# Attention output of an encoder block turned by VectorE and passed through HBM, in place of TensorE transposes

## The chip, the cores and the metric

The kernel runs on one core of a Trainium2 chip. The metric is the device time of one execution in microseconds; the time of the kernel before is the median of three runs. TensorE (PE in the profile) multiplies matrices, VectorE (DVE), ScalarE (ACT) and GpSimd (POOL) work on tiles in SBUF and PSUM, and SyncE (SP) issues the loads and stores. Each engine takes its instructions in the order of the program and waits on semaphores for the others.

## What is computed

One layer of a hybrid encoder, 1024 tokens by 1024 channels, all in float32. Cut to what bears on the change:

```
h    = rmsnorm(x);  proj = h @ w_in                  # 1024 x 5664
q, k, v, r, lr_f, lr_b, u, g_a, g_b = split(proj)
o    = gla(q, k, v, fwd) + gla(reversed, bwd)        # 4 heads, 128 keys, 256 values each
o    = o * rsqrt(mean(o*o over a head's 256 values) + EPS)
o    = o (heads side by side: 1024 x 1024) * gla_norm
o    = o * silu(r)
y_a  = o @ w_branch_gla
y_b  = pooling mixer of u
x    = x + (sigmoid(g_a)*y_a + sigmoid(g_b)*y_b) @ w_out
x    = x + swiglu ffn(rmsnorm(x));  return rmsnorm(x)
```

## The kernel before

Every float32 operand of a large product is split into a high and a low part, and a product is three matmuls (`products`, L273): high by high, high by low, low by high. `split_to` makes the parts: the cast of the high part on ACT (L200), the difference on POOL or DVE (L201). Weights are loaded as `raw` or `fraw` and become `wh` and `wl`. The larger products are cut further, in the manner of Strassen, into seven products p1 to p7 per pair of blocks (`Unit`, `Gates`): sums of weight blocks (`fs`, L1093, on DVE) are multiplied by sums of activation blocks. The latter lie in HBM (`f_out`), are reloaded as `hs` (L673) and split into `trh` (ACT, L707) and `trl` (DVE, L698).

The order of the work is written by hand, engine by engine. PE works through the large products; after each three matmuls `pump` moves generators on by what the matmuls are worth, so the attention's small steps stand between them. A value that a generator yields is how much PE work lies until its next step.

**Attention of a head** (`attention(h)`) first makes the decays (L822 onwards). Then come the backward states, then the output loop over eight chunks of 128 tokens (NT = 8, tokens on the partitions). A chunk's output bank `op` gets its terms on PE, the last of them from the forward state `sf` (L998). The state is brought on meanwhile by `advance`: `kv` on PE, `st` on DVE (L913), `sf` and `so` on ACT (L917, L921). DVE copies `op` into the SBUF tile `o` (L999; two tiles, four chunks of 256 values each), and ACT squares and sums it (L1000). After the last chunk `rms_scale` makes all eight chunks' scales `ors` (an addition on DVE, L304, a power on POOL). `normalize` (L1019), eight TENSOR_SCALAR, runs from the list `unscaled` at the next head's decay, and the two tiles are then put on the list `deferred`, from which `flush` (L563) issues stores to `o_out`. The last head is normalized at once and stays in SBUF.

**Behind the attention** PE makes the six first blocks of r (j = 0 to 5, two halves of 512 tokens each; channels on the partitions, tokens along the free axis). `load_o` (L1033) brings heads 0 to 2 back as `ol` at j = 2, 3 and 4. `gated(j, half, ...)` needs o with channels on the partitions. It takes silu of r on ACT (`sr`, L1185), turns four 128x128 blocks of o on PE into a PSUM bank `tp` (L1188), and DVE multiplies the bank by the gla_norm column and `sr` (L1195). The first three blocks of r are put by, so from j = 3 on each half gates two of them. Finished blocks go out to `ob_out`. Blocks 6 and 7 of r are gate unit 0, made in seven products in the order p1, p2, p6, p5, p3, p7, p4; p1, p6 and others share the PSUM bank `u`, which ACT or DVE take into `ga` (L1474 copies, L1479 adds) before PE goes on in it. `gated` of these two blocks stands further back, between them and the next units.

Of the kernel before, what the change touches and what calls it, by code (L numbers as in the profile page):

```python
# [10 lines left out]
F32 = mybir.dt.float32  # L11
# [4 lines left out]
ALU = mybir.AluOpType  # L16

P = 128
# [3 lines left out]
NT = SEQ // P  # L22
HALF = 512
HEADS = 4
DK = 128
DV = 256
RANK = 16
CH = 128
SUB = 64
GROUPS = 4  # L30
WINDOWS = (2, 4, 8, 16)
PAD = 8
# [21 lines left out]
def kernel(  # L54
# [20 lines left out]
    nc = tc.nc  # L75
# [10 lines left out]
    ps_g = ctx.enter_context(tc.tile_pool(name="ps_g", bufs=8 - MM_BANKS, space=bass.MemoryType.PSUM))  # L86

    dram = ctx.enter_context(tc.tile_pool(name="dram", bufs=1, space=bass.MemoryType.DRAM))
# [8 lines left out]
    def slot(dtype=F32, shape=(2, HALF), s="slot"):  # L97
        return slots.tile([P, *shape], dtype, tag="slot", name=name(s))
# [10 lines left out]
    def bank(pool, s="ps"):  # L109
        return pool.tile([P, HALF], F32, tag=pool.name, name=name(s))  # L110
# [5 lines left out]
    ident = const.tile([P, P], F32, tag="ident", name="ident")  # L116
# [185 lines left out]
    def rms_scale(ms, width, s):  # L302
        rs = vec(width, s)
        nc.vector.tensor_scalar(rs[:, :], ms, EPS, None, op0=ALU.add)  # L304
        nc.gpsimd.tensor_tensor(rs[:, :], rs[:, :], half_neg[:, :width], op=ALU.pow)
        return rs
# [132 lines left out]
    g_mix, g_ffn, g_gla, g_pool = (cols[:, 8 * i : 8 * i + 8] for i in range(4))  # L439
# [116 lines left out]
    deferred = []  # L556

    def later(dst, src):
        deferred.append((dst, src))

    def flush(eng=nc.sync):
        while deferred:
            eng.dma_start(*deferred.pop(0))  # L563
# [167 lines left out]
            aside.pop(0)  # L731


    o_heads, unscaled = {}, []
    HOLD, SCORES = 5.0, 6

    class ValueWeights:
# [75 lines left out]
    def attention(h):  # L813
# [16 lines left out]
        for run in runs:  # L830
            nc.scalar.activation(zs[run][:, :], zs[run][:, :], AF.Exp, scale=-1.0)
        if unscaled:
            unscaled.pop()()
        yield 3.5
        flush()
        for run in runs:
            nc.scalar.activation(zs[run][:, :], zs[run][:, :], AF.Ln, bias=1.0)
# [107 lines left out]
        q, k = qk_heads[h]  # L945
# [21 lines left out]
        for n in range(NT - 1, 0, -1):  # L967
            m = n - 1
# [9 lines left out]
        p = scores(0)  # L978
# [3 lines left out]
        o = [slot(shape=(4, DV), s="o") for _ in range(2)]  # L982
        ms = vec(NT, "oms")
        old = sf = None
        for n in range(NT):
            half, i = n // 4, n % 4
            op = bank(ps_g, "op")
            products(op[:, :DV], tokens(p, n), value(n), last=False)
            terms = []
            if n < NT - 1:  # L990
                terms.append((chunk_of(qe, n, 1), sb[half][:, i, :]))
            if n > 0:
                terms.append((chunk_of(qe, n, 0), sf[:, :]))
            for j, (a, b) in enumerate(terms):
                if j == len(terms) - 1 and n < NT - 1:
                    sf = s1((DV,), "sf")
                    old = advance(old, n, 0, kts[half, 0], sf[:, :], n == NT - 2)
                nc.tensor.matmul(op[:, :DV], a, b, start=False, stop=j == len(terms) - 1)  # L998
            nc.vector.tensor_copy(o[half][:, i, :], op[:, :DV])  # L999
            nc.scalar.activation(  # L1000
                op[:, DV:], op[:, :DV], AF.Square, scale=1.0 / 16.0, accum_out=ms[:, n : n + 1]
            )
            if n == 0:
                yield 0.38
                kts[1, 0] = transposed_keys(1, 0)
            if n == 1:
                yield 0.75
                q_next = scores(1)
            if n == 3:
                p = q_next  # L1010
            yield 1.02
        rs = rms_scale(ms[:, :], NT, "ors")
        if h == HEADS - 1:
            o_heads[h] = o

        def normalize():
            for n in range(NT):
                t = o[n // 4][:, n % 4, :]
                nc.vector.tensor_scalar(t, t, rs[:, n : n + 1], None, op0=ALU.mult)  # L1019
            if h < HEADS - 1:  # L1020
                for half in range(2):
                    later(o_out[h][:, 4 * half : 4 * half + 4, :], o[half][:, :, :])

        unscaled.append(normalize)
        if h == HEADS - 1:
            unscaled.pop()()

    o_out = [dram.tile([P, NT, DV], F32, name=f"o_out{h}") for h in range(HEADS - 1)]

    def load_o(h):  # L1030
        o_heads[h] = [slot(shape=(4, DV), s="ol") for _ in range(2)]
        for half in range(2):
            nc.sync.dma_start(o_heads[h][half][:, :, :], o_out[h][:, 4 * half : 4 * half + 4, :])  # L1033

    def sums_behind():
        prepare_beside(map(feature_sums, range(2)), 2)
# [145 lines left out]
    def gated(j, half, src):  # L1182

        sr = t2(s="sr")
        nc.scalar.activation(sr[:, :], src, AF.Silu)  # L1185
        tp = bank(ps_g, "tp")
        for i in range(4):
            nc.tensor.transpose(  # L1188
                tp[:, i * P : (i + 1) * P],
                o_heads[j // 2][half][:, i, (j % 2) * P : (j % 2 + 1) * P], ident[:, :],  # L1190
            )
        if j // 2 not in oT:
            oT[j // 2] = [slot(s="o") for _ in range(2)], []
        tiles, there = oT[j // 2]
        nc.vector.scalar_tensor_tensor(  # L1195
            tiles[half][:, j % 2, :], tp[:, :], g_gla[:, j : j + 1], sr[:, :], op0=ALU.mult, op1=ALU.mult
        )
        there.append((j, half))
        if len(there) == 4:
            c = j // 2 % 2  # L1200
            for half, t in enumerate(tiles):
                later(ob_out[j // 4, half][:, 2 * c : 2 * c + 2, :], t[:, :, :])
            soon(2, flush)
# [8 lines left out]
    for j in range(KT - 2):  # L1212
        if 2 <= j <= 4:
            load_o(j - 2)
        w = take()
        if j == 4:
            for _ in range(2):
                gunits[0].load()
        if j == 5:
            gates_ahead.step()  # L1220
        if j < BY:
            whole_r = slot(s="r")
        for half in range(2):
            if j >= BY and not sums_begun and (j > BY or not side):
                finish_side()
                finish_beside()
                prepare_beside([feature_parts()], 5)
                sums_begun = True
            ps = feature_major(w, hT, half)
            if half == 0:  # L1230
                flush()
            elif j == KT - 3:
                for _ in range(2):
                    gunits[1].load()
            if j < BY:
                nc.scalar.copy(whole_r[:, half, :], ps[:, :])
                raw_r.append((j, half, whole_r[:, half, :]))
            else:
                put_by()
                gated(j, half, ps[:, :])  # L1240
            if j == KT - 3 and half == 0:
                gates_ahead.step()
# [187 lines left out]
    def pooling():  # L1430

        for g in range(GROUPS):
            u = [t2(HALF + 2 * PAD, s="u") for _ in range(2)]
# [555 lines left out]
    scales = {}  # L1989
# [74 lines left out]
    for at, p in enumerate(OUT_ORDER):  # L2064
# [9 lines left out]
        for i in range(CLOSE if closing else n_of):  # L2074
            n = at * n_of + i
# [57 lines left out]
```

## Time and profile before

| | us |
|---|---|
| median of three runs | 1374.98 (1374.72 to 1375.22) |
| span of the profiled execution | 1373.4 |
| PE busy | 1361.4 |
| VectorE busy | 836.8 |
| ScalarE busy | 647.3 |
| GpSimd busy | 752.1 |
| DMA, mean busy share of 16 engines | 53.8% |

The profile is that of one execution. Its own time is its span and some 1.6 us around it, taking the median for it. The profile lists instructions as start, length, engine, line, operation, tile written and tiles read; "x2" joins two in a row, and square brackets show how long the engine had been idle and who released it. PE's lengths overlap: how much of PE a matmul takes is seen from one start to the next.

### The profile page before, as it was taken

How to read it: one execution, taken by the hardware profiler on the slowest of the kernel's cores; microseconds unless marked ns; L12 is line 12 of the kernel's file. 1: busy time of each engine (PE TensorE's matmuls, PEld its weight loads, DVE VectorE, ACT ScalarE, POOL GpSimd, SP SyncE). 2: the span in 40 equal slices, each digit the busy share in tenths (PEclk: the TensorE clock that was granted, in tenths of full speed). 3: DMA queues.
4: the chain of work that ended last, by engine and by line, in shares of the span. 5: the costliest groups of instructions: out<-in, count | busy, mean ns of one | idle time of the engine just before them, and what ended most of it. 6: DMA issues, size and time to landing. Idle time of an engine off the chain costs nothing. (4 is left out here: it accounts for less than half of the span.)

```text
span 1373.4 us, 17879 instructions
## 1 busy us (share of the span) xinstructions
PE 1361.4 (99%) x6310; PEld 1132.9 (82%) x6310; DVE 836.8 (61%) x1034; ACT 647.3 (47%) x1177; POOL 752.1 (55%) x557
## 2 busy tenths in 40 slices
PE   9999999999999999999999999999999999999998
PEld 7888888888888888888888888888888888888886
DVE  6974556554735777678883955655566556343375
ACT  7365666755534445554346533333333334444253
POOL 3323723222597547667764376666676667455454
PEclk9999999999999999999999999999999999999999
DMA  6321523314778569995416355555544447985451
GB/s 227 113 87 52 181 90 92 95 60 123 245 236 278 186 198 308 373 386 216 150 71 241 112 174 176 176 176 177 176 145 137 146 136 266 384 301 187 169 215 77
DMA packets 167834, 251.97 MB, mean 183 GB/s; under 512 B 11160, under 2 KB 94144, under 8 KB 167744
## 3 DMA queue, kind: packets, MB, share of 16 engines
q1 hardware_dynamic: 167600, 250.57, 53.8%
q8 instruction: 49, 0.80, 0.2%
q14 instruction: 41, 0.34, 0.1%
q10 hardware_dynamic: 144, 0.26, 0.0%
HBM read 168.74 MB, written 82.05 MB: 183 GB/s over the span
## 5 line engine op out<-in xcount | busy, mean ns | idle before, releaser
L201 POOL TENSOR_TENSOR wl<-fs,wh 128x512 fp32r<-128x512 f32 x124 | 173.1, 1400 | 163.5 <-ACT wh L200 104.0
L273 PE MATMUL ps<-gh,wh 128*128 128x512 f32 x616 | 240.5, 390 | 0.0
L273 PE MATMUL ps<-gl,wh 128*128 128x512 f32 x616 | 239.8, 389 | 0.3 <-DVE gl L1691 0.3
L273 PE MATMUL ps<-gh,wl 128*128 128x512 f32 x616 | 239.7, 389 | 0.0
L201 POOL TENSOR_TENSOR wl<-fraw,wh 128x512 fp32r<-128x512 f32 x93 | 134.0, 1442 | 75.0 <-ACT wh L200 72.4
L201 POOL TENSOR_TENSOR ol<-gor,oh 128x1024 fp32r<-128x1024 f32 (+1 forms) x42 | 101.3, 2417 | 86.0 <-ACT oh L200 71.7
L273 PE MATMUL ps<-hh,wh 128*128 128x512 f32 x356 | 145.1, 408 | 0.7 <-ACT ga L1474 0.7
L273 PE MATMUL ps<-hh,wl 128*128 128x512 f32 x356 | 139.0, 390 | 0.0
L273 PE MATMUL ps<-hl,wh 128*128 128x512 f32 x356 | 138.8, 390 | 0.0
L273 PEld LDWEIGHTS ps<-gl,wh 128*128 128x128 f32 x616 | 115.7, 188 | 24.5 <-DVE gl L1691 0.7
L273 PEld LDWEIGHTS ps<-gh,wh 128*128 128x128 f32 x616 | 115.7, 188 | 24.1 <-ACT hb L1710 0.2
L273 PEld LDWEIGHTS ps<-gh,wl 128*128 128x128 f32 x616 | 115.7, 188 | 23.9
L273 PE MATMUL ps<-oh,oh 128*128 128x512 f32 x308 | 119.8, 389 | 0.0
L273 PE MATMUL ps<-ol,oh 128*128 128x512 f32 x308 | 119.8, 389 | 0.0
L273 PE MATMUL ps<-oh,ol 128*128 128x512 f32 x308 | 119.8, 389 | 0.0
L201 POOL TENSOR_TENSOR wl<-wraw,wh 128x512 fp32r<-128x512 f32 x56 | 92.3, 1679 | 44.7 <-ACT wh L200 44.6
L201 POOL TENSOR_TENSOR wl<-raw,wh 128x512 fp32r<-128x512 f32 x34 | 47.4, 1404 | 108.3 <-ACT wh L200 71.9
L201 DVE TENSOR_TENSOR ol<-wor,oh 128x1024 fp32r<-128x1024 f32 (+1 forms) x42 | 62.8, 1506 | 68.1 <-ACT oh L200 55.5
L200 ACT CAST wh<-fs 128x512 fp32r<-128x512 f32 x124 | 76.1, 615 | 29.5 <-DVE fs L1093 28.3
L273 PEld LDWEIGHTS ps<-hh,wl 128*128 128x128 f32 x356 | 66.8, 188 | 14.4
L273 PEld LDWEIGHTS ps<-hh,wh 128*128 128x128 f32 x356 | 67.0, 188 | 13.1 <-ACT ga L1474 1.1
L273 PEld LDWEIGHTS ps<-hl,wh 128*128 128x128 f32 x356 | 67.0, 188 | 12.0
(281 smaller groups left out, 3073.4 us busy)
## 6 DMA issues: line engine op xcount, KB each, us to landing
fraw<-in_w_ffn_in_dram SPq DMA_DIRECT2D x44, 512.0 KB, 6.1
gor<-g_out SPq DMA_DIRECT2D x35, 512.0 KB, 6.1
fraw<-in_w_in_dram SPq DMA_DIRECT2D x22, 512.0 KB, 6.5
g_out<-s SPq DMA_DIRECT2D x44, 256.0 KB, 2.3
wor<-t_out SPq DMA_DIRECT2D x20, 512.0 KB, 3.7
raw<-in_w_in_dram SPq DMA_DIRECT2D x36, 256.0 KB, 5.1
g_out<-g SPq DMA_DIRECT2D x33, 256.0 KB, 2.6
x<-in_x_dram SPq DMA_DIRECT2D x16, 512.0 KB, 5.6
```

The costliest lines, as they stand in the source:

```text
L200: nc.scalar.copy(hi, src)
L201: eng.tensor_tensor(lo, src, as_f32(hi), op=ALU.subtract)
L273: nc.tensor.matmul(ps, a[i], b[j], start=first and n == 0, stop=last and n == 2, skip_group_check=onto)
```

## The change

The transposes leave TensorE. VectorE turns o in blocks of 32x32 with its own transpose, and the exchange of whole blocks is done by the addresses of the stores to HBM.

- In the output loop, chunk 3 is followed by `rms_scale` of the first four chunks, the end of the loop by that of the last four.
- `turn(half, part)` normalizes two chunks (two TENSOR_SCALAR of 128x256) and turns them with one transpose instruction into a tile `ot`. Half 0's two pieces stand behind chunks 5 and 6 in the loop. Half 1's stand beside the next head's decay, where `normalize` stood, with the yield of 3.5 there split into 2 and 1.5. In the last head they follow the loop.
- `o_out` now holds o with channels ahead of tokens, for all four heads. A half is stored by four DMAs of 32 partitions, and `load_o` reads a half as 128x2x512. The last head's stores are issued at j = 4, half 0, and it is reloaded at j = 5, half 0.
- `gated` reads `ol` with channels on the partitions. Tokens lie there in another order (32 by 32 interleaved), so DVE does the multiplication in four instructions of 128x4x32.

```diff
         if unscaled:
-            unscaled.pop()()
-        yield 3.5
+            unscaled.pop(0)()
+        yield 2
+        if unscaled:
+            unscaled.pop(0)()
+        yield 1.5
         flush()
...
+        def turn(half, part):
+            if part == 0:
+                turned[half] = slot(shape=(DV // SQ, 4 * SQ), s="ot")
+            two = slice(2 * part, 2 * part + 2)
+            for i in range(2 * part, 2 * part + 2):
+                t = o[half][:, i, :]
+                nc.vector.tensor_scalar(t, t, scales[half][:, i : i + 1], None, op0=ALU.mult)
+            nc.vector.transpose(
+                turned[half][:, :, :].rearrange("p k (n b) -> p n k b", b=SQ)[:, two],
+                o[half][:, two, :].rearrange("p n (k a) -> p n k a", a=SQ),
+            )
+            if part:
+                to = o_out[h][half].rearrange("(k a) (i m) -> i a k m", a=SQ, i=4)
+                for i in range(4):
+                    (last_o if h == HEADS - 1 else deferred).append((to[i], turned[half][i * SQ : (i + 1) * SQ, :, :]))
...
             if n == 3:
                 p = q_next
+                scales[0] = rms_scale(ms[:, :4], 4, "ors")
+            if n in (5, 6):
+                turn(0, n - 5)
             yield 1.02
-        rs = rms_scale(ms[:, :], NT, "ors")
+        scales[1] = rms_scale(ms[:, 4:], 4, "ors")
         if h == HEADS - 1:
-            o_heads[h] = o
...
+            turn(1, 0)
+            turn(1, 1)
+            return
+        unscaled.extend(partial(turn, 1, part) for part in range(2))
...
-            nc.sync.dma_start(o_heads[h][half][:, :, :], o_out[h][:, 4 * half : 4 * half + 4, :])
+            nc.sync.dma_start(o_heads[h][half][:, :, :], o_out[h][half].rearrange("(j p) t -> p j t", p=P))
...
-        tp = bank(ps_g, "tp")
-        for i in range(4):
-            nc.tensor.transpose(
-                tp[:, i * P : (i + 1) * P],
-                o_heads[j // 2][half][:, i, (j % 2) * P : (j % 2 + 1) * P], ident[:, :],
-            )
...
+        turned = o_heads[j // 2][half][:, j % 2, :].rearrange("p (i n b) -> p i n b", i=4, b=SQ)
+        for i in range(4):
+            nc.vector.scalar_tensor_tensor(
+                every(tiles[half][:, j % 2, :], i), turned[:, i], g_gla[:, j : j + 1], every(sr[:, :], i),
+                op0=ALU.mult, op1=ALU.mult,
+            )
...
             if half == 0:
                 flush()
+                if j == 4:
+                    deferred.extend(last_o)
+                    flush()
+                elif j == 5:
+                    load_o(HEADS - 1)
```

The order shows three places. First PE between the two halves of the sixth block of r (j = 5), where two gated operations stood; `hh` and `hl` are the parts of h, `wh` and `wl` those of the weights. Before:

```order
L273 MATMUL ps_3497<-hl_313,wh_3411 128x512
L273 MATMUL ps_3497<-hh_312,wl_3412 128x512
L1188 MATMUL tp_3538<-ident,ol_3151 128x128 x4
L1188 MATMUL tp_3546<-ident,ol_3376 128x128 x4
L273 MATMUL ps_3560<-hh_494,wh_3401 128x512
L273 MATMUL ps_3560<-hl_495,wh_3401 128x512
L273 MATMUL ps_3560<-hh_494,wl_3402 128x512
```

And in the changed program:

```order
L274 MATMUL ps_3544<-hl_313,wh_3458 128x512
L274 MATMUL ps_3544<-hh_312,wl_3459 128x512
L274 MATMUL ps_3607<-hh_494,wh_3448 128x512
L274 MATMUL ps_3607<-hl_495,wh_3448 128x512
L274 MATMUL ps_3607<-hh_494,wl_3449 128x512
```

The two rows of four transposes are gone, here and wherever they stood, and nothing takes their place; the matmuls around them keep their order.

Second DVE at the last chunks of the output loop of head 3 and behind it. Before, from the copy of chunk 5 on:

```order
L999 COPY o_3102<-op_3248 128x256
L913 SCALAR_TENSOR_TENSOR st_3283<-kv_3279,fac_2933,so_3261 128x256
L999 COPY o_3102<-op_3273 128x256
L999 COPY o_3102<-op_3292 128x256
L304 TENSOR_SCALAR ors_3302<-oms_3103 128x8
L1019 TENSOR_SCALAR o_3101<-o_3101,ors_3302 128x256 x4
L1019 TENSOR_SCALAR o_3102<-o_3102,ors_3302 128x256 x4
```

And in the changed program, from the copy of chunk 5 on:

```order
L1021 COPY o_3148<-op_3297 128x256
L997 TENSOR_SCALAR o_3147<-o_3147,ors_3266 128x256 x2
L998 STREAM_TRANSPOSE ot_3315<-o_3147 128x2x8x32
L917 SCALAR_TENSOR_TENSOR st_3336<-kv_3332,fac_2979,so_3310 128x256
L1021 COPY o_3148<-op_3326 128x256
L997 TENSOR_SCALAR o_3147<-o_3147,ors_3266 128x256 x2
L998 STREAM_TRANSPOSE ot_3315<-o_3147 128x2x8x32
L1021 COPY o_3148<-op_3348 128x256
L305 TENSOR_SCALAR ors_3358<-oms_3149 128x4
L997 TENSOR_SCALAR o_3148<-o_3148,ors_3358 128x256 x2
```

A piece now stands ahead of the last `st` and another ahead of the last copy. The other two follow the loop.

Third SP, which issues the DMAs of j = 4 and 5. Before:

```order
L673 DMA hs_3463<-f_out_562 128x1024
L673 DMA hs_3505<-f_out_564 128x1024
L563 DMA ob_out_2740<-o_3320 128x1024
L563 DMA ob_out_2741<-o_3321 128x1024
L673 DMA hs_3528<-f_out_564 128x1024
L673 DMA hs_3574<-f_out_561 128x1024
L673 DMA hs_3595<-f_out_561 128x1024
L1085 DMA fraw_3597<-in_w_in_dram 128x8x128
```

And in the changed program:

```order
L564 DMA o_out_568<-ot_3315 32x8x128 x4
L564 DMA o_out_568<-ot_3361 32x8x128 x4
L674 DMA hs_3514<-f_out_562 128x1024
L674 DMA hs_3552<-f_out_564 128x1024
L564 DMA ob_out_2777<-o_3370 128x1024
L564 DMA ob_out_2778<-o_3371 128x1024
L674 DMA hs_3575<-f_out_564 128x1024
L1050 DMA ol_3583<-o_out_568 128x2x512
L1050 DMA ol_3584<-o_out_568 128x2x512
L674 DMA hs_3621<-f_out_561 128x1024
L674 DMA hs_3642<-f_out_561 128x1024
L1102 DMA fraw_3644<-in_w_in_dram 128x8x128
```

The last head's eight stores stand ahead of the first of these `hs` loads, and its two reloads behind the third; the other loads and stores keep their order.

More of the change, by code (lines that the diff above doesn't have):

```diff
@@ L29 @@
 SUB = 64
+SQ = 32
 GROUPS = 4
@@ L731, in finish_beside @@
             aside.pop(0)
-    o_heads, unscaled = {}, []
+    o_heads, unscaled, last_o = {}, [], []
     HOLD, SCORES = 5.0, 6
@@ L984, in attention @@
         old = sf = None
+        scales, turned = {}, {}
+        def turn(half, part):
[13 more added lines that the diff above has]
+                    (last_o if h == HEADS - 1 else deferred).append((to[i], turned[half][i * SQ : (i + 1) * SQ, :, :]))
         for n in range(NT):
@@ L1010, in attention @@
                 p = q_next
+                scales[0] = rms_scale(ms[:, :4], 4, "ors")
+            if n in (5, 6):
+                turn(0, n - 5)
             yield 1.02
-        rs = rms_scale(ms[:, :], NT, "ors")
+        scales[1] = rms_scale(ms[:, 4:], 4, "ors")
         if h == HEADS - 1:
-            o_heads[h] = o
[L1016 to L1028, printed above, removed]
+            turn(1, 0)
+            turn(1, 1)
+            return
+        unscaled.extend(partial(turn, 1, part) for part in range(2))
+    o_out = [dram.tile([2, DV, HALF], F32, name=f"o_out{h}") for h in range(HEADS)]
     def load_o(h):
-        o_heads[h] = [slot(shape=(4, DV), s="ol") for _ in range(2)]
+        o_heads[h] = [slot(s="ol") for _ in range(2)]
         for half in range(2):
-            nc.sync.dma_start(o_heads[h][half][:, :, :], o_out[h][:, 4 * half : 4 * half + 4, :])
+            nc.sync.dma_start(o_heads[h][half][:, :, :], o_out[h][half].rearrange("(j p) t -> p j t", p=P))
     def sums_behind():
@@ L1194, in gated, with every @@
         tiles, there = oT[j // 2]
-        nc.vector.scalar_tensor_tensor(
-            tiles[half][:, j % 2, :], tp[:, :], g_gla[:, j : j + 1], sr[:, :], op0=ALU.mult, op1=ALU.mult
-        )
+        def every(t, i):
+            return t.rearrange("p (n i b) -> p i n b", n=4, b=SQ)[:, i]
+        turned = o_heads[j // 2][half][:, j % 2, :].rearrange("p (i n b) -> p i n b", i=4, b=SQ)
[4 more added lines that the diff above has]
+            )
         there.append((j, half))
```

## The prediction, made before the changed kernel ran

> **What bounds the kernel now.** I read the page's busy shares and slices first, then the answers for the tiles of the output path, then the stretch in which they run, instruction by instruction on each engine.
>
> ```profile
> span 1373.4 us, 17879 instructions
> PE 1361.4 (99%) x6310; PEld 1132.9 (82%) x6310; DVE 836.8 (61%) x1034; ACT 647.3 (47%) x1177; POOL 752.1 (55%) x557
> PEclk9999999999999999999999999999999999999999
> PE 44%; DVE 1%; ACT 1%; issue 0%; POOLq 0%; POOL 0%; DVEq 0%; ACTq 0%
> ```
>
> TensorE (PE) is busy 99% of the span at a full granted clock, and the chain that ended last is nearly all PE. So a PE instruction that goes is time gained, until PE reaches something that isn't ready. The profiled span is 1373.4 us and the median of the runs 1374.98; the 1.6 us between them lies around the span and stays. A measurement of this kernel can tell about 0.2% (2.75 us) from no change.
>
> **What goes.** Answer for the tile `tp` (min/median/max in ns, first and last start), then the PE timeline at one place of each size (start, length, instruction):
>
> ```profile
> L1188 PE MATMUL tp<-ident,ol x48: 272/273/273, 319.9 to 352.5; 128*128 128x128 f32 x48
> L1188 PE MATMUL tp<-ident,o x16: 270/272/273, 360.8 to 382.6; 128*128 128x128 f32 x16
> L1195 DVE SCALAR_TENSOR_TENSOR o<-tp,cols,sr x16: 740/748/751, 324.5 to 383.0; 128x512 f32<-128x512 f32 x16
>   DVE o L1195: 18.5, 5
> ```
> ```profile
> 319.91 1.04 PE L1188 MATMUL tp<-ident,ol 128*128 128x128 f32 x8
> 320.70 0.47 PE L273 MATMUL ps<-hh,wh 128*128 128x512 f32 x1
> 321.02 0.39 PE L273 MATMUL ps<-hl,wh 128*128 128x512 f32 x1
> 321.25 0.40 PE L273 MATMUL ps<-hh,wl 128*128 128x512 f32 x1
> ```
> ```profile
> 360.83 0.60 PE L1188 MATMUL tp<-ident,o 128*128 128x128 f32 x4
> ...
> 361.50 0.39 PE L273 MATMUL ps<-trl,wh 128*128 128x512 f32 x1
> ```
>
> Matmuls overlap, so I count starts. A 128x512 matmul takes 0.23 us from start to start (321.02 to 321.25). The eight transposes and the matmul behind them take 319.91 to 321.02, 1.11 us, so the eight cost 0.88; the four at 360.83 cost 0.67 - 0.23 = 0.44. The 48 `ol` transposes stand in six groups of eight, the 16 `o` ones in four groups of four: 6 x 0.88 + 4 x 0.44 = **7.0 us** leave PE. All of it counts only if PE waits nowhere else; the 18.5 us that VectorE (DVE) waited for `tp` was its own idle time.
>
> **What is added on DVE, in the output loop.** A piece of `turn` is two TENSOR_SCALAR of 128x256 and one transpose of 512 elements per partition. Half 0's two pieces stand behind the `o` copies of chunks 5 and 6. Here are those chunks of head 3, on DVE, ScalarE (ACT) and PE, then the nearest durations:
>
> ```profile
> 315.70 0.41 DVE L999 COPY o<-op 128x256 f32<-128x256 f32 x1
> 317.56 0.48 DVE L913 SCALAR_TENSOR_TENSOR st<-kv,fac,so 128x256 f32<-128x256 f32 x1 [1.45 <-ACT op L1000]
> 317.96 0.41 DVE L999 COPY o<-op 128x256 f32<-128x256 f32 x1
> 319.41 0.42 DVE L999 COPY o<-op 128x256 f32<-128x256 f32 x1 [1.04 <-PE op L998]
> ```
> ```profile
> 318.08 0.51 ACT L917 ACTIVATE sf<-st,fac 128x256 f32<-128x256 f32 x1 [0.45 <-DVE st L913]
> ```
> ```profile
> 318.78 0.60 PE L998 MATMUL op<-sf,qe 128*128 128x256 f32 x2
> ```
> ```profile
> L1019 DVE TENSOR_SCALAR o<-o,ors x32: 343/348/1374, 134.3 to 324.2; 128x256 f32<-128x256 f32 x32
> ```
> ```profile
> L881 DVE TENSOR_TENSOR ke<-z,k 128x512 f32<-128x512 f32 x16 | 10.9, 682 | 3.1 <-ACT z L872 3.1
> L851 DVE TENSOR_TENSOR_SCAN z<-carry,la x8: 1232/1806/2296, 86.0 to 283.0; 128x512 f32<-128x512 bf16 x8
> ```
>
> DVE idles 1.45 us ahead of the last `st`; `sf` follows and ends at 318.59, 0.19 before PE takes it at 318.78. So the piece of chunk 5 may last about 1.6 us before PE waits. The second piece has 1.04 us before the last copy, which no PE instruction of the loop waits for. No row shows this transpose. [...] Two TENSOR_SCALAR at 0.35 come to it, less the overlap that the rows show (`st` runs 0.08 past the next start): a piece is 1.2 to 1.8 us. I take the transpose at 0.7, since it is nearest to a plain pass over one tile, and the piece at 1.3: no PE wait in heads 0, 2 and 3. At the upper end each of them loses 0.2.
>
> [...] No row here shows the transpose itself.
>
> Head 1 is tighter, since DVE splits `vl` in that loop:
>
> ```profile
> 190.65 0.41 DVE L999 COPY o<-op 128x256 f32<-128x256 f32 x1
> 191.74 0.48 DVE L913 SCALAR_TENSOR_TENSOR st<-kv,fac,so 128x256 f32<-128x256 f32 x1 [0.68 <-ACT so L921]
> ```
>
> There 0.68 us is idle, so with the same 0.19 behind it a piece of 1.3 costs PE 1.3 - 0.87 = **0.4 us** (0.3 at a piece of 1.2, 0.9 at 1.8). The split `rms_scale` after chunk 3 lies in the same kind of gap. Half 1's pieces replace the eight TENSOR_SCALAR that stood beside the next head's decay already; DVE has gaps there, and I cost them at nothing. For head 3 they run before the first gated operation, which no longer has to wait for PE.
>
> **The gated operation.** One 128x512 from PSUM becomes four of 128 elements from SBUF. The `st` at 317.56 is 256 elements and the next starts 0.40 later; two of 512 start 1.33 apart per pair (353.86 to 355.19 below), 0.665 each. Linear in the elements, 128 take 0.27, so four take 1.08 in place of 0.665: +0.42 us per gated operation, 16 times, +6.7 us of DVE. Upper end: these now read both inputs from SBUF as `fs` does, and `fs` takes 1.42 here against 0.682 for `ke`, the same shape and kind, when VectorE and GpSimd (POOL) work together; doubled, a gated operation would cost +1.5. The busy times by stretch say where that is hidden (start:end, length, then PE, weight loads, DVE, ACT and POOL, the clock, the DMA share and GB/s):
>
> ```profile
> 320.00:346.00 26.00, 26.00 (x135) 21.87 (x134) 10.69 (x19) 10.55 (x17) 5.50 (x4) 1.00 0.27 83
> 346.00:351.00 5.00, 5.00 (x25) 4.18 (x24) 4.12 (x5) 3.52 (x5) 1.30 (x1) 1.00 0.96 330
> 351.00:363.00 12.00, 12.00 (x60) 9.99 (x60) 11.79 (x10) 8.72 (x14) 8.24 (x5) 1.00 0.99 344
> ```
>
> Up to 346 us most of DVE's time is idle. From 351 to 363 it has nothing left, and what that does comes next.
>
> [...]
>
> **Where PE meets the next wait.** Behind the six groups of eight, PE does products p1 and p2 of gate unit 0 and then p6, whose bank must be copied out by ACT first. The rows of before at this place:
>
> ```profile
> 347.32 2.81 SPq L673 DMA_DIRECT2D hs<-f_out  x3
> ```
> ```profile
> 352.11 1.05 ACT L707 CAST trh<-hs 128x1024 fp32r<-128x1024 f32 x1 [2.13 <-DMA hs<-f_out]
> 353.06 0.63 ACT L1185 ACTIVATE sr<-r 128x512 f32<-128x512 f32 x1
> ...
> 356.64 0.62 ACT L200 CAST wh<-fs 128x512 fp32r<-128x512 f32 x1 [1.44 <-DVE fs L1093]
> 357.16 0.58 ACT L1474 COPY ga<-ps 128x512 f32<-128x512 f32 x1
> ```
> ```profile
> 353.86 1.41 DVE L1195 SCALAR_TENSOR_TENSOR o<-tp,cols,sr 128x512 f32<-128x512 f32 x2
> 355.19 1.42 DVE L1093 TENSOR_TENSOR fs<-fraw,fs 128x512 f32<-128x512 f32 x1
> ```
> ```profile
> 346.17 0.47 PE L273 MATMUL ps<-hh,wh 128*128 128x512 f32 x1
> ...
> 348.79 0.39 PE L273 MATMUL ps<-hh,wl 128*128 128x512 f32 x1
> ...
> 358.10 0.39 PE L273 MATMUL ps<-trh,wh 128*128 128x512 f32 x1
> 364.86 0.50 PE L273 MATMUL ps<-hh,wh 128*128 128x512 f32 x1 [0.68 <-ACT ga L1474]
> ```
>
> Read as a chain: the `hs` load issued at 347.32 lands just before 352.11 (4.8 us); ACT casts it, then makes `sr`; DVE runs two gated operations and `fs`; ACT casts that as `wh`, then copies p1's bank, done at 357.74. PE starts p6 at 358.10, 0.36 later: no wait, but only just in time. That chain has no transpose in it, so it doesn't get shorter by itself.
>
> In the changed program PE reaches p6 six groups earlier, at 358.10 - 5.28 = 352.8. There the matching `hs` load takes a slot whose last reader is PE's 12th matmul of the product that began at 346.17; that matmul ended at 348.79 + 0.39 = 349.18 before, and ends five groups (4.40) earlier now, at 344.8. Plus 4.8 the load lands at 349.6, 2.5 earlier than before. The chain behind it is longer by two gated operations, 2 x 0.42 = 0.84. So p1's copy ends at 357.74 - 2.5 + 0.84 = 356.1, and PE **waits some 3.3 us** at p6, of which before had none. At the ends: 4.8 if the load lands 1 us later and the gated operations contend, 0 if the load finds its slot elsewhere.
>
> Behind p6, the wait at 364.86 is PE itself finishing a bank, ACT copying it and PE going on; it stays. The four groups of four (1.76, in the 7.0 already) are gained if DVE keeps up: it was full from 351 to 363 and gets +0.42 per gated operation.
>
> **Through HBM.** A half's store is now four DMAs in place of one, and the last head's eight stores and two loads are new; all are issued by SyncE (SP), in order, between other loads:
>
> ```profile
> L673 SPq DMA_DIRECT2D hs<-f_out x8: 319/320/1996, 296.2 to 349.8; - x8
> ```
>
> At 0.32 us an issue a half's four take 1.3 us. The last head's eight stand ahead of an `hs` load two before the one above; I cost them at nothing, with 1.3 for the upper end, if they delay the chain to p6. The store (1 MB) falls into the stretch up to 346 us with a DMA share of 0.27, which is room enough; the reload (1 MB) is issued behind the `hs` load of the chain, into the stretch at 0.96 to 0.99. At its 344 GB/s it takes 3.0 us, by which the `fraw` loads behind it land later. I cost that at nothing too, as p6 holds PE back by about as much, and at 1 us for the upper end.
>
> **Sum.** On the profiled span: -7.0 + 0.4 (head 1) + 3.3 (p6) = -3.3, so 1370.1; with the 1.6 around it, 1374.98 - 3.3 = **1371.7 us**.
>
> **Rivals.**
> 1. *All of it is gained*: `hs` lands in time or p1's copy isn't held by it. Then 7.0 less 0 to 0.4: 1368.0 to 1368.4. For it: the load is released by PE, which is early too. Against: in before the whole chain ended only 0.36 us ahead of PE. 0.2.
> 2. *DVE becomes the bound from 346 to 367 us*: the gated operations at twice their price behind busy DVE push `fs` and the `ga` additions; six of them up to there at +1.1 more, the part that isn't idle about half, +3.3: near 1375.0, no change. 0.2.
> 3. *The transpose is slow, and the loop waits* (slower): every head has one piece ahead of the last `st`; it decides from a transpose of about 1.0 us on, and each further microsecond costs PE 4 (one per head). At 2.6 us, twice the scan's fastest row, that is 4 x 1.6 + 0.7 (head 1's smaller gap) = 7.1, and with p6's 3.3 the time is 1374.98 - 7.0 + 7.1 + 3.3 = 1378.4. For it: 4-byte data written in runs of 32 elements, which no row shows. Against: the slowest kind of row with 512 elements that stands here, the scan, does it in 1.23 at best. 0.1.
> 4. *The change doesn't do what it says*, that is, transposes stay on PE: the order of the changed program has none left in this stretch, so I give it nothing.
>
> **How the numbers follow.** The forecast (wait at p6 of 2.3 to 4.3 us) has 0.5 and its own range 1370.5 to 1373.0. Below 1372.2 (0.2%) lie rival 1 and some two thirds of the forecast: faster 0.53. Rival 2 and the rest of the forecast are within 0.2%: 0.37. Slower, above 1377.7: 0.10. The range takes in rival 1 and most of rival 2: 1367.9 to 1376.0.
>
> **What would show it.** No `tp` on PE, and PE starts from 320 to 352 us closed up by 0.88 per group. A PE idle of about 3.3 us ahead of p6, put down to ACT `ga`; rival 1 shows none. The transpose's own row, below 1.0 us; a PE wait at the last `sf` of head 1 alone (rival 3: in all four heads). The gated rows at about 0.3 us. Wrong if PE idle appears elsewhere, on `wl` or `fraw` beyond 367 us, because DMA or POOL were paced to the old PE.

## The result, and the profile after

| | us |
|---|---|
| before, median of 19 runs | 1375.01 (1374.69 to 1375.78) |
| changed, median of 19 runs | 1377.34 (1376.68 to 1378.67) |
| ratio, 95% interval | 1.0018 (1.0011 to 1.0025) |
| span of the profiled execution | 1375.6 (before 1373.4) |

The change cost 2.3 us where 3.3 were to be gained. From the page of the changed kernel:

```profile
PE 1357.9 (99%) x6246; PEld 1129.0 (82%) x6246; DVE 861.7 (63%) x1102; ACT 647.2 (47%) x1177; POOL 756.6 (55%) x561
PEclk9999999999899999999999999999999999999999
```

The 64 transposes are gone from PE, and its busy time fell by 3.5 us, yet the span grew. One slice of the granted clock has a digit below 9, which before had nowhere: the slice from 344 to 378 us. Here is PE's timeline there:

```profile
352.03 0.39 PE L274 MATMUL ps<-hh,wl 128*128 128x512 f32 x1
359.66 0.79 PE L274 MATMUL ps<-trh,wh 128*128 128x512 f32 x1 [7.25 <-ACT ga L1497]
360.25 0.63 PE L274 MATMUL ps<-trl,wh 128*128 128x512 f32 x1
360.68 0.63 PE L274 MATMUL ps<-trh,wl 128*128 128x512 f32 x1
...
365.37 0.47 PE L274 MATMUL ps<-trl,wh 128*128 128x512 f32 x1
365.68 0.40 PE L274 MATMUL ps<-trh,wl 128*128 128x512 f32 x1
...
368.79 0.50 PE L274 MATMUL ps<-hh,wh 128*128 128x512 f32 x1 [0.68 <-ACT ga L1497]
```

Two things are new. PE waits 7.25 us ahead of p6 for ACT's copy of p1's bank. And the matmuls behind the wait start 0.43 us apart (360.25 to 360.68) where 0.23 is usual, until about 365.5. The busy times of that stretch (start:end, length, PE, weight loads, DVE, ACT, POOL, clock, DMA share, GB/s), first after, then before:

```profile
356.00:362.00 6.00, 2.34 (x6) 1.86 (x7) 5.64 (x9) 3.50 (x6) 4.00 (x3) 0.50 1.10 355
```
```profile
356.00:362.00 6.00, 6.00 (x30) 4.95 (x30) 6.00 (x5) 4.62 (x7) 6.00 (x5) 1.00 1.07 383
```

The granted clock was 0.50 after and 1.00 before, with PE idle for most of the earlier part of that window. Matching the starts of PE's matmuls one by one gives the account:

| stretch, by PE starts | before | after | difference |
|---|---|---|---|
| start to p1's first matmul | 352.54 | 346.81 | -5.73 |
| p1's first matmul to p6's first | 5.57 | 12.85 | +7.28 |
| p6's first to p3's first | 6.76 | 9.13 | +2.37 |
| p3's first to the last | 1001.86 | 1000.38 | -1.48 |

That is +2.44 up to PE's last matmul in the two profiled executions (their spans differ by 2.2), close to the 2.33 between the medians. The third row contains one group of four `o` transposes (0.44) that is gone, so the slow clock cost 2.37 + 0.44 = 2.8 us. The first holds the six groups of eight, head 1's loss (below), and 0.57 by which this execution of the changed kernel was ahead by 178 us. Of that, 0.45 is a wait that this execution of before had and this one has not:

```profile
166.77 0.50 PE L273 MATMUL ps<-wl,hh 128*128 128x512 f32 x1 [0.44 <-POOL wl L201]
```

That is luck of the one execution: in the profiled executions of the eleven variants of the changed kernel below, PE idles 0.47 to 1.17 us at this place.

The chain that PE waited for, on SP, ACT, DVE and POOL of the changed kernel:

```profile
332.05 10.99 SPq L674 DMA_DIRECT2D hs<-f_out  x2
343.09 0.90 SPq L564 DMA_DIRECT2D ob_out<-o  x2
344.29 1.10 SPq L674 DMA_DIRECT2D hs<-f_out  x1
345.44 1.96 SPq L1050 DMA_DIRECT2D ol<-o_out  x2
```
```profile
352.02 1.05 ACT L708 CAST trh<-hs 128x1024 fp32r<-128x1024 f32 x1 [3.68 <-DMA hs<-f_out]
...
358.50 0.62 ACT L201 CAST wh<-fs 128x512 fp32r<-128x512 f32 x1 [3.40 <-DVE fs L1110]
359.03 0.58 ACT L1497 COPY ga<-ps 128x512 f32<-128x512 f32 x1
```
```profile
353.63 4.24 DVE L1212 SCALAR_TENSOR_TENSOR o<-ol,cols,sr 128x128 f32<-128x128 f32 x8 [1.09 <-ACT sr L1202]
357.79 0.68 DVE L1110 TENSOR_TENSOR fs<-fraw,fs 128x512 f32<-128x512 f32 x1
```
```profile
354.66 2.53 POOL L202 TENSOR_TENSOR wl<-fs,wh 128x512 fp32r<-128x512 f32 x2 [6.66 <-ACT wh L201]
```

The sixth `hs` load was issued at 344.29, 3.0 us earlier than before (347.32), and was cast at 352.02, 0.1 us earlier: it took 7.7 us in place of 4.8. The fifth load, second in the first row, left SP only at about 342.7; two stores, the sixth load and the two reloads followed within 5 us. In before the fifth load and the two stores left at the same time (342.85 to 343.7), but the sixth load only 3.6 us behind them. Then two gated operations took DVE 4.24 us where they took 1.41 before, while POOL made `wl`.

The transpose itself and the place in head 1 where PE lost time:

```profile
L998 DVE STREAM_TRANSPOSE ot<-o x16: 711/712/715, 126.7 to 324.0; 128x512 f32<-128x512 f32 x16
```
```profile
192.28 0.28 PE L274 MATMUL op<-vh,p 128*128 128x256 f32 x1
192.67 0.70 PE L1020 MATMUL op<-sf,qe 128*128 128x256 f32 x2
```

The transpose lasts 0.71 us. In head 1 the last `sf` matmul starts 0.39 behind the one ahead of it where it was 0.11 (192.85 to 192.96) before, a loss of 0.28; the other heads lose nothing.

### The profile page after: what moved, and what is told of

Read it like the earlier page. It is cut to its first block, busy times and chain, and to the rows that moved or that the text cites. A ratio compares the mean times of both kernels' runs of the same rounds, so it can differ in the third digit from the quotient of the medians.

```text
span 1375.6 us, 17848 instructions
## 1 busy us (share of the span) xinstructions
PE 1357.9 (99%) x6246; PEld 1129.0 (82%) x6246; DVE 861.7 (63%) x1102; ACT 647.2 (47%) x1177; POOL 756.6 (55%) x561
```

## The experiments

All edits are to the changed kernel, except in one run that says otherwise. The theory: PE idles at p6 since p1's copy stands in ACT's queue behind the cast of a `wh` that needs DVE, DVE is behind the gated operations, and these behind a late load; the idle then costs clock too. This table collects all runs (us; each kernel's own profiled execution for the three distances, the median of its runs, and the ratio to the kernel before on the same chip):

| kernel | p1 to p6 | p6 to p3 | p3 to end | median | ratio (95%) |
|---|---|---|---|---|---|
| before | 5.57 | 6.76 | 1001.86 | 1375.01 | |
| changed | 12.85 | 9.13 | 1000.38 | 1377.34 | 1.0018 (1.0011 to 1.0025) |
| reload_later | 11.88 | 7.97 | 1000.38 | 1376.55 | 1.0012 (1.0002 to 1.0021) |
| copy_first | 8.16 | 9.07 | 1000.40 | 1373.36 | 0.9990 (0.9980 to 0.9999) |
| warm | 12.72 | 6.41 | 1000.34 | 1375.30 | 1.0002 (0.9992 to 1.0011) |
| dense_stt | 10.88 | 8.70 | 1000.34 | 1375.49 | 1.0012 (0.9994 to 1.0030) |
| early_issue | 10.65 | 8.42 | 1000.34 | 1375.40 | 1.0001 (0.9992 to 1.0010) |
| early_first | 5.44 | 9.80 | 1002.01 | 1372.99 | 0.9984 (0.9975 to 0.9993) |
| before_first | 5.57 | 7.13 | 1001.81 | 1375.50 | 1.0003 (0.9994 to 1.0012) |
| all_late | 7.19 | 10.56 | 1001.93 | 1375.39 | 1.0001 (0.9992 to 1.0010) |
| first_late | 8.20 | 10.56 | 1001.94 | 1374.95 | 1.0002 (0.9993 to 1.0011) |
| dense_all | 5.44 | 10.90 | 1000.36 | 1372.55 | 0.9983 (0.9974 to 0.9992) |
| sr_psum | 10.57 | 8.19 | 1000.31 | 1374.82 | 1.0000 (0.9991 to 1.0010) |
| sr_all | 5.44 | 8.39 | 1001.95 | 1371.65 | 0.9973 (0.9963 to 0.9982) |

5.44 from p1 to p6 is no wait at all.

**The reload behind the loop (reload_later).** Is it the last head's reload that delays the `hs` load?

```diff
-                elif j == 5:
-                    load_o(HEADS - 1)
...
+    load_o(HEADS - 1)
     for p, i, half in ((1, 0, 0), (2, 1, 0), (3, 1, 1)):
```

> Only the last head's two reloads are moved: behind the loads of the next gate unit instead of between the hs loads. Theory: these 1 MB share the DMA engines with the hs load on which the wait at p6 hangs. Then that load (issued near 344.3, its cast at 352.0 in the changed kernel) lands 1.5 to 3 us earlier, the cast starts at 349 to 350.5, PE's wait at p6 falls from 7.25 to 4.5 to 5.8 us, and the median comes down by 1.5 to 3 us, to 1374.3 to 1375.8. Rival: the transfers issued ahead of it (two ob_out stores of 512 KB) hold it back; then the cast stays at 352.0 within 0.3, the wait at 7.0 to 7.4, and the median at 1377.3 within 0.5.

The wait at p6 fell by 0.97 and the median by 0.8: the reload is a small part of it. Something ahead of the load must count as well.

**p1's copy ahead of the weights (copy_first).** The chain is left as it is, but ACT's copy no longer stands behind it.

```diff
-    for _ in range(AHEAD - 2):
-        gates_ahead.step()
     flush()
...
+            if n == at == 0:
+                zs[of].run(p)
+                for _ in range(AHEAD - 2):
+                    gates_ahead.step()
             if not gates_ahead.step() and at in (5, 7):
                 line_make()
-            zs[of].run(p)
+            if n or at:
+                zs[of].run(p)
```

> Only the order at gate unit 0 is changed: p1 and ACT's copy of its bank come ahead of the preparation of the weights of p6 and p5, so that the copy no longer stands behind the cast that waits for DVE's two last gated operations and fs. Theory: p6 waits for that copy and nothing else; the copy then follows the sr at 354 us and ends near 354.6, and p6 starts when its own weights are ready, at 356 to 357 instead of 359.66; the wait falls from 7.25 to 4 to 5 us and the median by 2.5 to 4 us, to 1373.3 to 1374.8. Rival: p6 needs something that comes as late by itself (trl or its weights through DVE); then p6 starts at 359 or later and the median stays at 1377.3 within 0.6.

ACT's and PE's timelines of this run:

```profile
357.86 0.58 ACT L1497 COPY ga<-ps 128x512 f32<-128x512 f32 x1
```
```profile
359.00 0.63 PE L274 MATMUL ps<-trh,wh 128*128 128x512 f32 x1 [2.56 <-ACT wh L201]
...
360.36 0.80 PE L274 MATMUL ps<-trh,wl 128*128 128x512 f32 x1 [0.30 <-POOL wl L202]
```

The copy now runs straight behind `sr`, and PE waits 2.56 for its weights in place of 7.25. The median fell by 4.0 us, to below before. So what ended PE's wait was the place of the copy in ACT's queue. What is left is a wait for `wh`; that it comes of the late load is not shown by this run alone, but it is gone in early_first below, where the load is early. (This profiled execution was some 4 us late ahead of the place; only distances are read from it.)

**The clock (warm).** Sixty 128x128 transposes with an output that nothing reads keep PE at work during the wait.

```diff
+            if n == 0 and p == 6:
+                dummy = bank(ps_g, "dummy")
+                for i in range(60):
+                    nc.tensor.transpose(dummy[:, :P], ident[:, :], ident[:, :])
             zs[of].run(p)
```

> Sixty transposes of the identity into a spare bank are added ahead of p6, work that no result uses, about 6.5 us of PE inside the 7.25 us wait. Theory: the matmuls from 359.7 to 365.7 start 0.43 apart instead of 0.23 because the clock granted to PE fell in the idle time; with PE busy the clock row shows full speed there, p6 still starts near 359.7, the matmuls behind it start 0.23 apart, and the median falls by 2.4 to 2.8 us, to 1374.5 to 1375. Rival: those matmuls are slow for another reason (a transfer or the load of their operands); then they stay at 0.43 and the median at 1377.3 within 0.4.

```profile
353.07 6.71 PE L1560 MATMUL dummy<-ident 128*128 128x128 f32 x60
360.35 0.50 PE L274 MATMUL ps<-trh,wh 128*128 128x512 f32 x1 [0.57 <-ACT ga L1497]
360.69 0.40 PE L274 MATMUL ps<-trl,wh 128*128 128x512 f32 x1
360.92 0.39 PE L274 MATMUL ps<-trh,wl 128*128 128x512 f32 x1
```

p6 starts no earlier, but its matmuls are 0.23 apart from the second on, and p6 to p3 fell from 9.13 to 6.41. So the slow matmuls behind the wait come of PE's idleness, and not of the data or the weights. The median fell by 2.0 and not by 2.7. The profiled execution of the changed kernel isn't typical in two ways that offset each other: it lacks the wait at 167 us (its p1 began at 346.81, warm's at 347.63), and its slow stretch is the longest. Against warm's 6.41 the five profiled executions with waits of 5.0 to 7.25 us ahead of p6 lost 1.6 to 2.7 us there; their granted clock was 0.50 for 10.2 us in the changed kernel's and for 6.8 us in the other four.

**One gated operation in place of four (dense_stt).**

```diff
-        for i in range(4):
-            nc.vector.scalar_tensor_tensor(
-                every(tiles[half][:, j % 2, :], i), turned[:, i], g_gla[:, j : j + 1], every(sr[:, :], i),
+        nc.vector.scalar_tensor_tensor(
+            tiles[half][:, j % 2, :], o_heads[j // 2][half][:, j % 2, :], g_gla[:, j : j + 1], sr[:, :],
```

> Each gated operation is one DVE instruction of 128x512 that reads ol and sr from SBUF as they lie, instead of four of 128x4x32; the tokens of the attention output stay in the interleaved order, so the sum over the reordering is left out of the result. Theory: the last two gated operations took 4.24 us (353.63 to 357.87) where two instructions from PSUM took 1.41 before; as two dense ones they take 1.4 to 2.2, the copy of p1 and p6 come 2 to 2.8 us earlier (p6 at 357 to 357.7), and the median falls by 2 to 3.5 us. Rival: only the late load counts; then p6 moves by less than 0.7 and the median by less than 0.9.

```profile
354.08 1.42 DVE L1211 SCALAR_TENSOR_TENSOR o<-ol,cols,sr 128x512 f32<-128x512 f32 x2 [1.63 <-ACT sr L1202]
355.41 1.75 DVE L1110 TENSOR_TENSOR fs<-fraw,fs 128x512 f32<-128x512 f32 x1
```

The two operations take 1.42 again, and the wait fell by 1.97. But `fs` behind them now takes 1.75 where it took 0.68: it now runs beside POOL, at work on four `wl` from 355.11 on (7.10 us), which in the changed kernel had just finished two (354.66 + 2.53) when `fs` began. Part of the hold-up moved to the next instruction.

**The load issued earlier (early_issue).** Tiles share slots that are handed out in turn. Four unused slots, taken ahead of the fifth `hs` load, give that load a slot whose readers are done, and SP is not blocked on it.

```diff
+                if len(wholes) == 4:
+                    for _ in range(4):
+                        nc.gpsimd.memset(slot(s="pad")[:, 0, :2], 0.0)
                 wholes.append(slot(s="hs"))
```

> Four tiny POOL memsets on spare slots are added ahead of the fifth hs load, so that this load no longer takes a slot that PE reads until the last product of r. Theory: in the changed kernel that load blocked SP until 342.70, and two ob_out stores, ready at 339, and the hs load of the chain (344.29) left in one burst of 512 KB transfers, so that the chain's load took 7.7 us. With the slot free SP issues the fifth load at 333 and the two stores near 339, the chain's load still leaves at 343 to 344.5 but lands by 348.5, its cast starts at 347 to 349 instead of 352.0, p6 starts 2.5 to 4 us earlier, and the median falls by 2.5 to 5 us. Rival: the landing is set by something else (the bandwidth of HBM at this place, the two reloads); then the cast stays within 0.7 of 352.0 and the median within 0.9 of 1377.3.

SP, ACT and DVE of this run (it is 1.0 us later than the changed kernel's throughout):

```profile
333.10 0.81 SPq L677 DMA_DIRECT2D hs<-f_out  x2
333.97 2.70 SPq L564 DMA_DIRECT2D ob_out<-o  x2
345.26 0.32 SPq L677 DMA_DIRECT2D hs<-f_out  x1
345.68 0.89 SPq L1053 DMA_DIRECT2D ol<-o_out  x2
```
```profile
349.53 1.05 ACT L711 CAST trh<-hs 128x1024 fp32r<-128x1024 f32 x1 [1.87 <-DMA hs<-f_out]
```
```profile
350.23 2.35 DVE L702 TENSOR_TENSOR trl<-hs,trh 128x1024 fp32r<-128x1024 f32 x2
352.50 4.22 DVE L1215 SCALAR_TENSOR_TENSOR o<-ol,cols,sr 128x128 f32<-128x128 f32 x8
```

The fourth and fifth loads leave at 333, the stores behind them at 334 and 336, and the sixth load takes 345.26 to 349.53, 4.3 us. So the 7.7 were the burst, and most of it what went just ahead of the load, the fifth load and two stores; the two reloads still follow it at once. The cast came 3.5 earlier in the run's own time, but the wait fell by only 2.2 and the median by 1.9, less than the theory wanted: `trl`, and behind it the gated operations, now hold the chain on DVE.

**Both (early_first), and copy_first on the kernel before (before_first).**

> The free slot for the fifth hs load and the earlier copy of p1's bank (the edit of copy_first) together. Theory: both causes of the wait at p6 are gone; the copy follows sr near 351, PE waits 0 to 1.5 us at p6, the clock stays at full, and of the seven microseconds of the transposes 5.5 to 6.5 are gained against the kernel before: 1368.5 to 1369.7. Rival: DVE, full with the gated operations, fs and trl from 346 to 362, becomes the bound further on (p2's addition, p5, p3); then the wait moves behind p6 and the median stays above 1371.

> The edit of copy_first alone on the kernel before, where PE did not wait at p6. Theory: nothing to gain there, 1375.0 within 0.4, so that what copy_first gains belongs to the wait that the change made. Rival: the new order is better for every version (it would also shorten the wait of 0.68 us ahead of p3); then 1373.5 or less.

early_first has no wait at p6. PE's timeline shows where the wait went:

```profile
363.06 0.66 PE L274 MATMUL ps<-hh,wh 128*128 128x512 f32 x1 [3.75 <-ACT ga L1500]
363.52 0.63 PE L274 MATMUL ps<-hl,wh 128*128 128x512 f32 x1
```

3.75 us ahead of p3, again for a copy behind late weights, and again with slow matmuls behind it. 1372.99 is 2.2 us below before, but not the 1368 of everything gained: the wait moved, as the rival had it. On the kernel before the same edit gives nothing (1375.50), so the gain isn't one that before had lying about.

**The last pair of gated operations put off (all_late, first_late).** From early_first and from copy_first: `gated` for j = 5, half 1, runs behind p1's copy and the weights.

```diff
-                put_by()
-                gated(j, half, ps[:, :])
+                if j == KT - 3 and half:
+                    held = [raw_r.pop(0), (j, half, ps[:, :])]
+                else:
+                    put_by()
+                    gated(j, half, ps[:, :])
```

> early_first, and the last two gated operations of r's sixth block (two sr on ACT, eight instructions on DVE) are issued behind the copy of p1 and the weights of p6, p5 and p3 instead of ahead of them. In early_first PE no longer waited at p6 but 3.75 us ahead of p3, for ACT's copy of p5, which stood behind a cast that waited 4.4 us for DVE's eight gated instructions (352.47 to 356.73). Theory: DVE's gated work in ACT's way is the second limit; out of the way the wait ahead of p3 falls to 0.7 to 2 us and the median to 1369.5 to 1371.5. Rival: it is the sum of DVE's work that counts, and p2's addition on DVE, behind the gated operations, now holds ACT in the same way; then the wait stays above 3 us and the median at 1373 within 0.6.

> The same order without the spare slots (the fifth hs load blocks SP again, the chain's load lands near 352). Theory: the casts of hs stand ahead of p1's copy on ACT, so the copy ends near 353.7 and p6 starts about 354 to 354.8, a wait of 2 to 2.5 us; median 1371.3 to 1373. Rival: with the gated operations moved the load no longer matters; then it equals all_late within 0.5.

Both missed. ACT and PE of all_late:

```profile
353.75 0.59 ACT L1503 COPY ga<-ps 128x512 f32<-128x512 f32 x1 [3.49 <-DVE fs L1113]
```
```profile
354.90 0.50 PE L274 MATMUL ps<-trh,wh 128*128 128x512 f32 x1 [1.59 <-ACT wh L201]
...
356.31 0.79 PE L274 MATMUL ps<-trh,wl 128*128 128x512 f32 x1 [0.68 <-POOL wl L202]
...
365.46 0.50 PE L274 MATMUL ps<-hh,wh 128*128 128x512 f32 x1 [2.53 <-ACT ga L1503]
```

The copy moved and with it the order in which slots are taken; ACT now idles 3.49 us ahead of it, until DVE has read a `fraw` for an `fs`. That the copy's tile takes the slot of that `fraw` is inferred and was not tried. p6 waits for weights (1.59, and 0.68 behind its first matmuls), p3 still waits 2.53, and behind both the matmuls start 0.43 apart for a while. first_late has the same two places with 2.60 and 2.55, and its median lies within 0.5 of all_late's, as its rival had it. Putting work off moved the wait and did not remove it.

**What holds DVE up (dense_all, sr_psum, sr_all).** dense_all is early_first with dense_stt's edit. sr_psum keeps the four short operations, but puts `sr` into a PSUM bank, so that each reads one SBUF tile. sr_all is sr_psum and early_first together.

```diff
-        sr = t2(s="sr")
+        sr = bank(ps_g, "sr")
```

> early_first with each gated operation as one DVE instruction of 128x512 from SBUF (the tokens stay interleaved; the sum over the reordering is left out of the result, as in dense_stt). Theory: the eight short instructions cost 2.8 us more than two dense ones at 352 to 357 us, and that is what holds ACT and PE ahead of p3; the wait of 3.75 falls to 0.7 to 2 and the median from 1373.0 to 1369.5 to 1371.5. Rival: what the gated operations save, fs and trl lose to POOL, as in dense_stt, where fs rose from 0.68 to 1.75; then the wait stays above 2.5 and the median above 1372.

> One word of the changed kernel is changed: sr, the second input of the gated operations, lies in a PSUM bank (the one that the transposes used before) instead of SBUF. Theory: DVE and POOL hold each other up where a DVE instruction reads two tiles in SBUF; before, the gated operation read one from PSUM and took 0.75 beside POOL as without it. With sr in PSUM the last eight short instructions (4.24 us from 353.63) take 2.2 to 2.8, p6 starts 1.3 to 2.2 us earlier against the changed kernel, and the median falls by 1.3 to 2.5, to 1374.8 to 1376.0. Rival: they are slow because they are short and start behind the semaphores of ACT; then they still take over 3.8 and the median stays at 1377.3 within 0.6.

> sr in PSUM together with early_first (spare slots, earlier copy of p1's bank). Theory: in early_first the eight short instructions (4.26 us) held ACT and with it p5's copy ahead of p3, a wait of 3.75; with 1.5 to 2 us less there the wait falls to 1.5 to 2.3, the clock stays up, and the median falls from 1373.0 to 1369.3 to 1371.3. Rival: as in dense_all, what DVE gains POOL loses (its four wl took 8.46 there) and PE waits for wl; then the median stays above 1372.

The gated rows by form: changed, dense_stt, sr_psum (out<-in xcount, busy us, mean ns, idle ahead):

```profile
L1212 DVE SCALAR_TENSOR_TENSOR o<-ol,cols,sr 128x128 f32<-128x128 f32 x64 | 28.6, 516 | 13.2 <-ACT sr L1202 10.6 <-POOL wl L202 2.4
```
```profile
L1211 DVE SCALAR_TENSOR_TENSOR o<-ol,cols,sr 128x512 f32<-128x512 f32 x16 | 14.2, 915 | 16.3 <-ACT sr L1202 15.0 <-POOL wl L202 1.2
```
```profile
L1212 DVE SCALAR_TENSOR_TENSOR o<-ol,cols,sr 128x128 f32<-128x128 f32 x64 | 17.4, 342 | 15.4 <-ACT sr L1202 14.2 <-POOL wl L202 1.2
```

Then DVE of sr_psum at the place, and POOL of dense_all:

```profile
354.09 2.16 DVE L1212 SCALAR_TENSOR_TENSOR o<-ol,cols,sr 128x128 f32<-128x128 f32 x8 [1.76 <-ACT sr L1202]
```
```profile
353.71 8.46 POOL L202 TENSOR_TENSOR wl<-fs,wh 128x512 fp32r<-128x512 f32 x4 [4.58 <-ACT wh L201]
```

With one input in PSUM eight short operations take 2.16, 0.27 each; with both in SBUF, 4.24. So it isn't their number that costs, but the second SBUF input while POOL works. The sum hides how: looked at one by one, six of the eight in the changed kernel last 0.34 to 0.35 us each, and these two do not:

```profile
354.68 1.39 DVE L1212 SCALAR_TENSOR_TENSOR o<-ol,cols,sr 128x128 f32<-128x128 f32 x1
356.00 1.35 DVE L1212 SCALAR_TENSOR_TENSOR o<-ol,cols,sr 128x128 f32<-128x128 f32 x1
```

POOL's two `wl` of the row at 354.66 further up begin at 354.66 and 355.88, last 1.26 and 1.31, and end about 0.15 us ahead of these two operations. So these two, started beside a `wl`, lasted until it was done. Of all 64 in the changed kernel, 53 last 0.31 to 0.35 and 11 from 1.0 to 1.4; each of the 11 starts beside a `wl` or a `wsum` of POOL and ends 0.14 to 0.15 us behind it. Their mean of 516 ns is the length of none.

In dense_all DVE runs at its own pace for longer (two gated operations in 1.41, `fs` in 0.69) and POOL loses: four `wl` take 8.46, the first of them, with DVE at work beside it without a pause, 3.76; the changed kernel has two in 2.53. PE then waits 2.80 for that `wl` behind p6's start, until 357.53, so the time is only 0.4 us below early_first's and above the 1371.5 expected, as the rival had it. sr_psum fell by 2.5 us, as expected.

sr_all, 1371.65, is 3.5 us below before and the fastest, just above what was expected. Its PE:

```profile
361.21 0.64 PE L274 MATMUL ps<-hh,wh 128*128 128x512 f32 x1 [2.35 <-ACT ga L1500]
361.64 0.63 PE L274 MATMUL ps<-hl,wh 128*128 128x512 f32 x1
...
364.63 0.49 PE L274 MATMUL ps<-hh,wl 128*128 128x512 f32 x1
364.96 0.40 PE L274 MATMUL ps<-hh,wh 128*128 128x512 f32 x1
```

What it leaves behind is a wait of 2.35 ahead of p3, and 1.6 us of slow clock behind that (1001.95 against 1000.38 from p3 to the end).

## Why the prediction was wrong

- **What leaves PE: right.** 7.0 predicted. Measured are 0.93 per group of eight (5.73 + 0.28 - 0.57, with 0.12 that falls just behind p1's first matmul, is 5.56) and 0.44 + 1.48 for the four groups of four: 7.5.
- **DVE's piece in the output loop: right.** 0.7 for the transpose and 1.3 for a piece, out of 1.2 to 1.8, were estimates from the rows of `ke` (0.682) and of the scan (1.232 at best); no row of before shows this transpose. 0.71 and, in most of the 16 pieces, 1.27 to the start of the next instruction were measured in the changed kernel. Head 1 lost 0.28 (predicted 0.4), the others nothing. The rival of a slow transpose fell.
- **PE meets the next wait at p6: the place was right, the size was not.** The step that failed is "plus 4.8 the load lands at 349.6". The issue came as predicted (344.29 for 344.8), but the load took 7.7. The prediction carried over the duration of a load that SP had sent 3.6 us behind the second of the two stores (343.69 and 347.32 in before, 343.61 and 344.29 after); issued earlier, it stood right among them. early_issue shows the same load at 4.3. That is 2.4 us of the wait.
- **The gated operations: mis-sized.** +0.42 each was taken and +1.5 kept as the upper end; measured is (4.24 - 1.41) / 2 = +1.4. sr_psum gives the 0.27 per 128 elements that was worked out, so the linear term held. Contention with POOL, which the row of `fs` had shown (1.42, and 0.682 for `ke`), should have been in the value taken. It isn't a doubling of each operation, though: two of the eight wait out a `wl`, and that the upper end of +1.5 has the right size is luck in how many `wl` fell there. `fs` itself gained (0.68 in place of 1.42), POOL being idle by then. From the cast to the end of p1's copy it is 359.61 - 352.02 = 7.6 us, 2.0 more than before's 5.6; 0.84 were predicted, so 1.1 more. PE also came to p6 half a microsecond earlier than predicted. Together 3.3 + 2.4 + 1.1 + 0.5 = 7.3, where 7.25 stands.
- **A term was missing: the clock.** The prediction read a clock of 1.00 in every row of before and carried it through a wait that before didn't have. It cost 2.8 us in the profiled execution (warm's takes out 2.7 of them) and some 2.0 in the medians. With the wait's extra 4.0 that is 6.8; less 0.5 that the removal gave above its estimate, 0.1 in head 1 and the 0.57 of the other wait it is 5.6, the error of 1377.34 - 1371.7. This is a sum over two profiled executions; that it meets the medians to 0.1 is in part luck, as the 0.57 and the length of the slow stretch are the one execution's own.
- **"I cost them at nothing"** of the stores and the reload: reload_later gives 0.8 for the reload's place. The upper end of the wait, 4.8, took a load 1 us late together with the contention; the load was 2.4 late.
- **The rival of a busy DVE** had contention with POOL as its mechanism, priced as a doubling, but took it to act by itself. dense_stt and sr_psum give 1.9 and 2.5 us for it, behind a load that was late.

What stays open: which of the slots' readers blocked the fifth load is read from the order of slots and from SP's row, and shown only so far as another slot took the block away. early_issue and sr_psum together, without copy_first, were not run. The wait at 167 us is longer in the eleven variants (0.47 to 1.17) than in the two executions of the kernel before (0.44, and 0.24 in before_first); whether the change lengthens it was not tried.

## What to carry to other kernels

When an engine that sets the time loses work, look for the first wait behind it, and price that wait by what the chain will meet at its new time, not by the durations it had at its old one: a load moved into a burst takes the burst's time (here 7.7 us, and 4.3 out of it). If the wait is of some microseconds on PE, add a term for the clock behind it (here 1.6 to 2.7 us behind waits of 5.0 to 7.25). An operand that moves from PSUM to SBUF on DVE isn't free if POOL is at work there (here eight operations took 4.24 us, and 2.16 with `sr` in PSUM); look at its instructions one by one, as a mean hides the few that wait, and try the other operand in PSUM. And put a copy that frees a bank ahead of queued work that waits for something else.

## What the runs showed of the hardware

- **The clock.** Behind an idle of 7.25 (changed), 3.75 (early_first), 2.56 (copy_first) and 2.35 us (sr_all) PE's matmuls started 0.43 apart; in the changed kernel, where that lasted from 359.66 to 365.4, a granted clock of 0.50 was read. In sr_all it lasted only to 364.6. The wait of 0.68 ahead of p3 in the changed kernel was followed by 0.23, and so was copy_first's of 1.41 there; in all_late 1.59 and, two matmuls later, 0.68 were followed by 0.43. Which of these two waits did it, or both, was not tried. By the clock's record the fall came 2.0 (sr_psum, idle from 353.19, fall at 355.2) to 3.9 us (early_first, 359.31 and 363.2) after PE had gone idle, even when PE was at work again: in sr_all PE started at 361.21 and the clock fell at 361.4. In sr_all 2.35 us of idle were enough.
- **DVE beside POOL.** DVE instructions with two SBUF inputs and POOL's `wl` held each other up, and which one paid differed: in the changed kernel two of the eight short operations wait out a `wl` each (1.39 and 1.35 for 0.34) while POOL keeps its 1.26 to 1.31 per `wl`; in dense_all DVE's long ones mostly keep their pace (two gated operations 1.41, `fs` 0.69, `trl` 1.22, the next `trl` 1.66) and one `wl` takes 3.76, from 353.71 on; in dense_stt `fs` takes 1.75 and four `wl` 7.10. With one SBUF input the gated operations weren't held up: before's 16, from PSUM and SBUF, took 0.74 to 0.75 each, ten of them with POOL at work beside them, and sr_psum's 64 last 342 ns in the mean, the eight above 2.16 us with a `wl` beside them from 355.16 on.
- **A burst of loads.** The same 512 KB load took 7.7 us to its cast right behind another load and two stores (changed), 4.8 when SP had sent these 3.6 to 4.5 us ahead (before), and 4.3 when 9 to 12 us ahead (early_issue).
